# A two-layer hybrid attention and HGRN2 step: one modulation vector moved to VectorE, lower rates of modulation tiles on TensorE, scan and norm steps reordered

## The chip, the core and the metric

The kernel runs on one core of a Trainium2 chip. Its time is the device time of one execution in microseconds (us); for the kernel before, three runs gave 2567.06, 2569.72 and 2571.58, so the median is 2569.72. The profile comes from one further execution.

Five engines have queues of their own: TensorE (PE; its weight loads are listed apart as PEld), VectorE (DVE), ScalarE (ACT), GpSimd (POOL) and SyncE (SP). The last two only issue transfers here.

## What is computed

Two groups of 128 tokens (g = 0, context; g = 1, latent) go through two layers of width 2048. All numbers are float32.

```python
def hybrid_layer(x, mods, ...):
    shift1, scale1, gate1, shift2, scale2, gate2 = mods   # silu(c) @ w_mod[l] + b_mod[l]
    h = modulate(x, shift1, scale1)                       # x * (1 + scale) + shift
    q, k, v, hq, hff, hfb, hi, hgt = split_in(h @ w_in_l)
    att = rms_norm(attend(q, k, v, sink_l), attn_g_l)
    hg, s_f, s_b = hgrn_mixer(hq, hff, hfb, hi, hgt, ...) # two scans over the tokens, in chunks of 32
    mix = jnp.concatenate([att, hg], -1) @ w_o_l
    x = layer_norm(ALPHA * x + gate1 * mix, ln_g_l[0], ln_b_l[0])
    ffn = sq_relu_mlp(modulate(x, shift2, scale2), w_up_l, w_down_l)
    x = layer_norm(ALPHA * x + gate2 * ffn, ln_g_l[1], ln_b_l[1])
```

The six modulation vectors of a layer are numbered v = 0 to 5 in the order shift1, scale1, gate1, shift2, scale2, gate2. Vector (0, 4) is scale2 of the first layer, the scale in front of its MLP. The outputs are x of both groups, the context's k and v, and the final states of both scans.

## The kernel before

**Weight tiles.** Each weight matrix is cut into units of 512 output columns, and a unit into tiles of 512 rows (kg = 0 to 3): 1 MB, loaded as two raw halves of 512 KB by SyncE (L1456) into ten buffers (`RAW_BUFS`). ScalarE rounds each half to float32r (`wh`, L1477), and VectorE subtracts that from the raw half (`wl`, L1490); a product is made of three matmuls, high by high, high by low and low by high. Four buffers each hold `wh` and `wl`, two tiles. Unit kinds are T and N (L462, L477) and W in the MLP (L489, L491); `mm_tile` runs one tile.

**Modulation tiles.** `w_mod` comes in tiles of 1 MB too, 16 for one vector. They are used in two ways. A `Mod` tile goes to TensorE (L204): four float32 matmuls with two stationary columns, which the trace records as eight. `mod_done` then copies the vector from PSUM, transposes it with four matmuls and adds the bias. A `ModH` tile goes to VectorE: four multiply-adds of 128x1024 into two accumulators (L269; the first product of each accumulator, two for a half vector, is ScalarE's, L267). A half vector has eight such tiles. `ModH.done` then sums over the partitions on TensorE with a matmul by ones (L278), copies, and transposes (L305). `POOLED` names the vectors that go the second way. The first layer's vectors 0 and 1 are made in quarters by `ModQ` (L224) ahead of all this.

**The order of the work.** `put_unit` writes a list of work, `seq`: the weight tiles in order, and between them modulation tiles by two credits. After each weight tile `RATE` is added to one credit and `PRATE` to the other, and for each whole credit one tile of `modseq` (TensorE) or of `poolseq` (VectorE) is put into the list:

```python
            pcredit[0] += prate
            while pcredit[0] >= 1.0:
                pcredit[0] -= 1.0
                if poolseq:
                    seq.append(("mod",) + poolseq.popleft())
```

The stages are r1 and r2 (the first and second 512 rows of the first layer's input projection, 13 weight tiles each), in (13 units: 26 tiles in the first layer, 52 in the second), o (two halves of four units with two tiles each: the first over the scan's part of the mix, the second over the attention's) and mlp (four rounds of four up and four down units, 128 tiles). `flush` puts all remaining tiles of the vectors that are needed next into the list at once; vectors 3 and 4 are flushed before the last unit of o. The raw halves are asked for in the order of the list.

**Tasks.** What follows a unit (attention, scans, norms) is written as generators. Each `yield` ends a step; `pump` runs one step of each of the first few admitted tasks, once in the middle of a weight tile and once after it. A task is admitted while at most four PSUM banks are promised. `need` runs steps until a task is done. `scan_task` makes the decayed products of q and k (L793, L794), the matmuls pI (L790), pX in three groups (L813, `across`) and pO. `att_fin` scales the attention output by its RMS (L679), transposes it (L683) and splits it for the output projection.

**The engines' order.** On GpSimd and SyncE the queue has the written order. On the other three a planner orders the instructions ahead of time, by written order among those that its cost model holds ready, so an instruction can stand earlier or later in the queue than where it was written. `ordered` switches to the written order on these three too, in the last tile of a layer half and the first unit after it (the closing). There `hole` puts up to five TensorE modulation tiles into the wait for the norm, and `ln_open` and `ln_mod` normalize and transpose (L973, L993, L1000) four blocks n, one ahead of each weight tile; a modulation tile that stands in the list between these weight tiles comes between these blocks. `ln_out` multiplies the normalized blocks by the norm's gain and adds its bias (L1120, L1121), from rows that GpSimd loads into the two buffers G (L1113, L1114).

## Time and profile before

| | |
|---|---|
| three runs, median (lowest, highest) | 2569.72 us (2567.06, 2571.58) |
| the profiled execution, its own time | 2570.34 us |
| its span, first to last instruction | 2568.6 us |
| mean granted TensorE clock | 0.988 |
| busy: PE, PEld | 2496.6, 2051.5 us |
| busy: DVE, ACT, POOL | 1884.7, 1269.1, 99.3 us |
| moved by DMA | 651.79 MB, mean 254 GB/s |

The span is the time between the first and the last instruction in the trace. Busy is the union of an engine's instructions; a matmul's end is modelled. A wait is idle time of an engine, put down to the instruction that released it. The stages begin, by the first matmul of their first weight tile, at 124.2 us (r2), 219.8 (in), 440.5 (o), 534.9 (second half of o), 596.5 (mlp), 1351.4 (in of the second layer), 1721.7 (o) and 1834.8 (mlp).

### The profile page before, as it was taken

To read this page: it belongs to the slowest core of one execution; us is meant where nothing else is said; L and a number is where in the kernel's file an instruction comes from. 1 tells how busy PE (TensorE), PEld (TensorE's weight loads), DVE (VectorE), ACT (ScalarE), POOL (GpSimd) and SP (SyncE) were. 2 spreads that over 40 slices of the span, in tenths; PEclk is the share of its full clock that TensorE was granted. 3 is DMA by queue.
4 is the path that set the end of the run, shared out by engine and by line. 5 is a ranking of instruction groups with operands and counts; after the bars stand their busy time and mean duration, and the time that the engine had idled before them with its cause. 6 is when DMAs were issued, how large, how long until landed. Compare 5 with 4: busy or idle time off the path is not lost.

```text
span 2568.6 us, 37718 instructions
## 1 busy us (share of the span) xinstructions
PE 2496.6 (97%) x14370; PEld 2051.5 (80%) x14370; DVE 1884.7 (73%) x2496; ACT 1269.1 (49%) x1867; POOL 99.3 (4%) x188
## 2 busy tenths in 40 slices
PE   7999999999999999999999989999999999999998
PEld 4787777668877877878878879797888888888886
DVE  3455787678997977987878788867876565666667
ACT  3434565435545545545535656644554454453552
POOL 2000000100000000000000010001010000000000
PEclk8999999999999999999999999999999999999999
DMA  9888878878887878888877666666666666666663
GB/s 360 283 287 321 293 263 300 288 262 314 312 295 275 309 271 277 293 281 287 278 251 278 205 220 223 209 223 201 207 232 208 225 206 228 209 211 229 205 228 105
DMA packets 192309, 651.79 MB, mean 254 GB/s; under 512 B 22928, under 2 KB 25552, under 8 KB 192128
## 3 DMA queue, kind: packets, MB, share of 16 engines
q1 hardware_dynamic: 177680, 614.56, 68.8%
q0 software_dynamic: 11504, 32.14, 4.2%
q10 hardware_dynamic: 2944, 2.69, 0.3%
q8 instruction: 112, 1.84, 0.3%
q14 instruction: 69, 0.57, 0.1%
HBM read 642.42 MB, written 6.88 MB: 253 GB/s over the span
## 4 chain that ended last, share of the span: by engine, by line
PE 50%; issue 42%; DMA 3%; DVE 3%; POOL 1%; ACT 1%; SPq 0%; DVEq 0%; POOLq 0%; ACTq 0%
PE acc L477 22%; PE acc L462 10%; PE acc L489 8%; PE acc L491 4%; PE psm L204 1%; PE psm L224 1%; DMA G<-in_lng_dram 1%; DMA raw<-in_w_mod_dram 1%; DVE wl L1490 1%; DMA out_nsf_dram<-lf 1%; PE pX L813 1%; POOL G L917 1%; PE pO L851 0%; DVE t L754 0%; PE pI L790 0%
## 5 line engine op out<-in xcount | busy, mean ns | idle before, releaser
L1477 ACT CAST wh<-raw 128x1024 fp32r<-128x1024 f32 x784 | 821.0, 1050 | 992.7 <-PE acc L477 468.7
L1490 DVE TENSOR_TENSOR wl<-raw,wh 128x1024 fp32r<-128x1024 f32 x784 | 951.1, 1220 | 390.1 <-ACT wh L1477 368.3
L269 DVE SCALAR_TENSOR_TENSOR ma<-raw,stat,ma 128x1024 f32<-128x1024 f32 x300 | 378.5, 1278 | 69.3 <-DMA raw<-in_w_mod_dram 68.5
L489 PE MATMUL acc<-ha,wh 128*128 128x512 f32 x960 | 345.5, 399 | 5.6 <-DVE t L1365 5.5
L489 PE MATMUL acc<-hb,wh 128*128 128x512 f32 x960 | 344.2, 398 | 0.0
L477 PE MATMUL acc<-wh,fa 128*128 128x512 f32 x1024 | 342.5, 390 | 0.0
L477 PE MATMUL acc<-wh,fb 128*128 128x512 f32 x1024 | 341.9, 390 | 0.0
L491 PE MATMUL acc<-ha,wl 128*128 128x256 f32 x960 | 269.4, 281 | 0.6 <-DVE wl L1490 0.5
L491 PE MATMUL acc<-hb,wl 128*128 128x256 f32 x960 | 269.4, 281 | 0.2 <-DVE wl L1490 0.2
L477 PEld LDWEIGHTS acc<-wh,fa 128*128 128x128 f32 x1024 | 192.2, 188 | 47.6 <-issue 5.2
L477 PEld LDWEIGHTS acc<-wh,fb 128*128 128x128 f32 x1024 | 192.2, 188 | 43.2 <-issue 3.4
L489 PEld LDWEIGHTS acc<-ha,wh 128*128 128x128 f32 x960 | 180.3, 188 | 56.6 <-DVE t L1365 6.9
L489 PEld LDWEIGHTS acc<-hb,wh 128*128 128x128 f32 x960 | 180.3, 188 | 46.9 <-issue 2.5
L462 PE MATMUL acc<-ha,wh 128*128 128x256 f32 x1152 | 211.7, 288 | 0.4 <-DVE ha L1015 0.4
L462 PE MATMUL acc<-hb,wh 128*128 128x256 f32 x1152 | 211.2, 287 | 0.0
L477 PE MATMUL acc<-wl,fb 128*128 128x512 f32 x512 | 199.5, 390 | 1.5 <-DVE wl L1490 1.5
L477 PE MATMUL acc<-wl,fa 128*128 128x512 f32 x512 | 199.3, 389 | 0.0
L462 PEld LDWEIGHTS acc<-ha,wh 128*128 128x128 f32 x1152 | 177.7, 192 | 25.6 <-issue 15.5
L491 PEld LDWEIGHTS acc<-ha,wl 128*128 128x128 f32 x960 | 181.3, 189 | 1.4 <-DVE wl L1490 1.3
L491 PEld LDWEIGHTS acc<-hb,wl 128*128 128x128 f32 x960 | 181.3, 189 | 0.5 <-DVE wl L1490 0.5
L462 PEld LDWEIGHTS acc<-hb,wh 128*128 128x128 f32 x1152 | 179.4, 195 | 1.3 <-issue 0.8
L462 PE MATMUL acc<-hb,wl 128*128 128x256 f32 x576 | 156.9, 285 | 0.0
(401 smaller groups left out, 3291.2 us busy)
## 6 DMA issues: line engine op xcount, KB each, us to landing
raw<-in_w_mod_dram SPq DMA_DIRECT2D x384, 512.0 KB
raw<-in_w_up_dram SPq DMA_DIRECT2D x256, 512.0 KB
raw<-in_w_down_dram SPq DMA_DIRECT2D x256, 512.0 KB
raw<-in_w_in_dram SPq DMA_DIRECT2D x208, 512.0 KB
raw<-in_w_o_dram SPq DMA_DIRECT2D x64, 512.0 KB
G<-gr POOLq DMA_DIRECT2D x48, 256.0 KB, 4.2
G<-in_lng_dram POOLq DMA_DIRECT2D x12, 256.0 KB, 4.9
G<-in_lnb_dram POOLq DMA_DIRECT2D x12, 256.0 KB, 5.0
```

The source lines that it names most:

```text
L204: pe.matmul(self.ps[32 * j:32 * j + 2, :], lhsT=stat[:, k, :], rhs=raw[j // 2][:, 512 * (j % 2):512 * (j % 2) + 512], start=k == 0, stop=k ...
L224: pe.matmul(self.ps[32 * j:32 * j + 2, :], lhsT=stat[:, 4 * k + j, :], rhs=raw[j // 2][:, 512 * (j % 2):512 * (j % 2) + 512], start=k == 0 ...
L269: dve.scalar_tensor_tensor(self.acc[g], raw[h], c, self.acc[g], ALU.mult, ALU.add)
L462: pe.matmul(ps, lhsT=(wh, wl)[w][k][:, 128 * m:128 * m + 128], rhs=x[:, t], start=f and k == 0 and m % 2 == 0 and (w, t) == (0, 0), stop=e ...
L477: pe.matmul(ps, lhsT=hl[k // 2][:, k % 2, t, gs], rhs=(wh, wl)[w][k], start=f and k == 0 and (t, w) == (0, 0), stop=e and k == ks[-1] == 3 ...
L489: pe.matmul(ps, lhsT=w0, rhs=x.rearrange("p a t -> p (a t)"), start=f and k == 0, stop=False, skip_group_check=True)
L491: pe.matmul(ps[:, 0:256], lhsT=w1, rhs=x[:, 0], start=False, stop=e and k == 3, skip_group_check=True)
L813: pe.matmul(pX[rows(ss), cols(m, ts)], lhsT=kd[:, cols(m, ss)], rhs=qb[:, cols(m, ts)], start=True, stop=True, tile_position=(0, 32 * ss.s ...
L917: side.dma_start(t, gr[g:g + 1, 512 * n:512 * n + 512].partition_broadcast(128))
L1477: act.copy(wh, r)
L1490: dve.tensor_tensor(wl, r, wh.bitcast(F32), ALU.subtract)
```

## The change

Vector (0, 4) joins `POOLED` as its first entry, and `PRATE` of r2, in and o of the first layer rises from 0 to 0.25. `RATE` falls in the first layer (in from 1.2 to 1.0, o from 1.2 to 0.65, mlp from 0.126 to 0.066) and in the second layer's in (0.13 to 0.06). In `scan_task` the two products qb and kd are made a step earlier, ahead of pI, and a step is put between the products at L829 and L830 and the third group of pX. In `att_fin` each block is scaled one block ahead of its transposition. In `ln_out` the rows of a block are loaded ten steps ahead of their use where it was six; the steps before the first block and between the blocks are fewer by as many.

```diff
--- before.py
+++ after.py
@@ -672,11 +672,20 @@
             dve.tensor_tensor(s, ssq[l, g][:, 0:1], ssq[l, g][:, 1:2], ALU.add)
             rs.append(rstd_of(s, 1, 1.0 / 1024, RMS_EPS))
         hls = [new_act("mx"), new_act("mx")]
-        pend = None
+        steps = [(j, g) for j in range(2) for g in range(2)]
+
+        def scaled(i):
+            j, g = steps[i]
+            at = att.pop((l, j, g))
+            dve.tensor_scalar(at, at, rs[g], None, ALU.mult)
+            return at
+
+        ahead = scaled(0)
         for j in range(2):
             for g in range(2):
-                at = att.pop((l, j, g))
-                dve.tensor_scalar(at, at, rs[g], None, ALU.mult)
+                at = ahead
+                if (j, g) != steps[-1]:
+                    ahead = scaled(2 * j + g + 1)
                 yield
                 pt = bank("pt")
                 for h in range(4):
@@ -784,15 +793,15 @@
         dve.tensor_tensor(e2, e2, k, ALU.mult)
         qe, ke = e1, e2
         yield
+        dve.tensor_tensor(eb, eb, q, ALU.mult)
+        dve.tensor_tensor(ed, ed, k, ALU.mult)
+        qb, kd = eb, ed
         yield
         pI = bank("pI")
         for m in range(4):
             pe.matmul(pI[:, 128 * m:128 * m + 128], lhsT=ke[:, 128 * m:128 * m + 128],
                       rhs=qe[:, 128 * m:128 * m + 128], start=True, stop=True)
         yield
-        dve.tensor_tensor(eb, eb, q, ALU.mult)
-        dve.tensor_tensor(ed, ed, k, ALU.mult)
-        qb, kd = eb, ed
         aT = e1
         dve.memset(aT, 0.0)
         mk = "f" if fwd else "b"
@@ -828,6 +837,7 @@
         yield
         dve.tensor_tensor(kdv[:, :, c0], kdv[:, :, c0], dm[:, :, c1:c1 + 1].to_broadcast([128, 4, 32]), ALU.mult)
         dve.tensor_tensor(qbv[:, :, c3], qbv[:, :, c3], dm[:, :, c2:c2 + 1].to_broadcast([128, 4, 32]), ALU.mult)
+        yield
         across(early, late)
         yield
         aTv = v3(aT, 4)
@@ -1106,13 +1116,13 @@
 
     def ln_out(key, li, sink_fn):
 
-        for _ in range(24):
+        for _ in range(20):
             yield
         for n in range(4):
             gt, bt = u("G"), u("G")
             side.dma_start(gt, a["lng"][li:li + 1, 512 * n:512 * n + 512].partition_broadcast(128))
             side.dma_start(bt, a["lnb"][li:li + 1, 512 * n:512 * n + 512].partition_broadcast(128))
-            for _ in range(6):
+            for _ in range(10):
                 yield
             for g in range(2):
                 y = yt.pop((key, n, g))
@@ -1120,16 +1130,16 @@
                     dve.tensor_tensor(y, y, gt, ALU.mult)
                     dve.tensor_tensor(y, y, bt, ALU.add)
                 sink_fn(n, g, y)
-                for _ in range(3):
+                for _ in range(1):
                     yield
 
 
     modseq = deque()
     poolseq = deque()
-    POOLED = ((0, 5), (1, 0), (1, 1), (1, 2), (1, 5))
+    POOLED = ((0, 4), (0, 5), (1, 0), (1, 1), (1, 2), (1, 5))
     ORDER = ['v0 h0 f0 b0 v1 h1 g0 f1 b1 g1 kv q0 q1'] * 2
     PARTS = [((2, 3), (0, 1))] * 2
-    PRATE = {(0, "r1"): 0, (0, "r2"): 0, (0, "in"): 0, (0, "o"): 0, (0, "mlp"): 0.45, (1, "in"): 0.178, (1, "o"): 0.05, (1, "mlp"): 0.135}
+    PRATE = {(0, "r1"): 0, (0, "r2"): 0.25, (0, "in"): 0.25, (0, "o"): 0.25, (0, "mlp"): 0.45, (1, "in"): 0.178, (1, "o"): 0.05, (1, "mlp"): 0.135}
     pcredit = [0.0]
     for l in range(L):
         for v in range(6):
@@ -1428,7 +1438,7 @@
             pump(3)
 
     GAP = 5
-    RATE = {(0, "in"): 1.2, (0, "o"): 1.2, (0, "mlp"): 0.126, (1, "in"): 0.13, (1, "o"): 0.456, (1, "mlp"): 0.066}
+    RATE = {(0, "in"): 1.0, (0, "o"): 0.65, (0, "mlp"): 0.066, (1, "in"): 0.06, (1, "o"): 0.456, (1, "mlp"): 0.066}
     for l in range(L):
         layer(l)
 
```

## Rows read from the trace of the kernel before

**Rows 1.** The page, part 1: busy us (share of the span) xinstructions of each engine.

```profile
PE 2496.6 (97%) x14370; PEld 2051.5 (80%) x14370; DVE 1884.7 (73%) x2496; ACT 1269.1 (49%) x1867; POOL 99.3 (4%) x188
```

**Rows 2.** Windows: stretch, length, PE, PEld, DVE, ACT, POOL busy (x), clock, DMA share, GB/s.

```profile
219.80:440.50 220.70, 214.33 (x1598) 170.45 (x1597) 162.32 (x302) 123.01 (x220) 10.53 (x20) 0.98 0.83 289
...
596.50:1351.40 754.90, 747.83 (x3908) 612.62 (x3908) 638.53 (x684) 373.60 (x476) 15.60 (x30) 1.00 0.83 287
1351.40:1721.70 370.30, 355.60 (x2560) 318.23 (x2560) 301.29 (x482) 226.23 (x392) 16.21 (x30) 0.98 0.66 228
```

**Rows 3.** Waits of PE: who <- for whom: us in total, times, longest us.

```profile
PE pX L813 <- DVE ed L830: 10.3, 2, 7.3
...
PE acc L489 <- DVE t L1365: 5.5, 3, 3.4
...
PE pt L683 <- DVE q L679: 4.1, 2, 2.2
...
PE pX L813 <- DVE s L824: 2.9, 2, 1.9
...
PE pt L993 <- DVE Z L973: 2.7, 1, 2.7
```

**Rows 4.** Timeline of PE: start, us, instruction, count [idle before <- releaser].

```profile
332.46 0.56 PE L813 MATMUL pX<-ed,t 128*32 128x32 f32 x16 [1.86 <-DVE s L824]
```

**Rows 5.** Windows after two holes.

```profile
333.00:336.40 3.40, 3.40 (x17) 3.40 (x17) 3.40 (x9) 0.63 (x1) 0.00 (x0) 0.50 0.51 188
...
1503.80:1514.00 10.20, 5.37 (x28) 5.25 (x29) 10.04 (x19) 3.18 (x8) 0.00 (x0) 0.50 0.43 153
```

**Rows 6.** Timeline of PE in the first layer's input projection.

```profile
245.71 0.28 PE L462 MATMUL acc<-hb,wl 128*128 128x256 f32 x1
245.92 1.04 PE L204 MATMUL psm<-raw,stat 128*2 128x512 f32 x8
246.89 0.50 PE L462 MATMUL acc<-ha,wh 128*128 128x256 f32 x2
247.23 0.28 PE L462 MATMUL acc<-ha,wl 128*128 128x256 f32 x1
247.35 0.40 PE L462 MATMUL acc<-ha,wh 128*128 128x256 f32 x2
...
252.62 0.28 PE L462 MATMUL acc<-hb,wl 128*128 128x256 f32 x1
252.83 1.90 PE L204 MATMUL psm<-raw,stat 128*2 128x512 f32 x16
254.65 0.50 PE L462 MATMUL acc<-ha,wh 128*128 128x256 f32 x2
```

**Rows 7.** Instructions by line and shape: xcount | busy us, mean ns | idle before.

```profile
L269 DVE SCALAR_TENSOR_TENSOR ma<-raw,stat,ma 128x1024 f32<-128x1024 f32 x300 | 378.5, 1278 | 69.3 <-DMA raw<-in_w_mod_dram 68.5 <-ACT ma L267 0.7
...
L278 PE MATMUL ph<-ma,ones 128*32 128x512 f32 x80 | 10.7, 605 | 0.0
...
L305 PE MATMUL pt<-ident,w 128*128 128x128 f32 x16 | 2.4, 272 | 0.0
```

**Rows 8.** Window of L204 alone: PE, PEld busy (x), clock, DMA share, GB/s.

```profile
514.60:534.30 19.70, 8.39 (x48) 1.06 (x48) 1.00 0.92 341
```

**Rows 9.** Windows of all instructions, columns as in rows 2.

```profile
369.00:392.50 23.50, 23.48 (x144) 16.07 (x140) 23.06 (x46) 15.16 (x29) 0.00 (x0) 1.00 0.81 282
...
534.90:579.60 44.70, 44.70 (x211) 34.54 (x210) 33.15 (x53) 16.41 (x20) 3.23 (x6) 0.97 0.71 228
...
650.00:700.00 50.00, 50.00 (x276) 42.10 (x275) 48.76 (x54) 27.11 (x38) 3.04 (x6) 1.00 0.87 310
```

**Rows 10.** Timeline of DVE in the second layer's first unit.

```profile
1358.95 4.86 DVE L269 SCALAR_TENSOR_TENSOR ma<-raw,stat,ma 128x1024 f32<-128x1024 f32 x4
```

**Rows 11.** Waits of DVE.

```profile
DVE Z L1120 <- DMA G<-in_lng_dram: 6.7, 2, 3.4
```

**Rows 12.** DMA issues: engine op xcount, KB each, median us to landing.

```profile
G<-in_lng_dram POOLq DMA_DIRECT2D x12, 256.0 KB, 4.9
```

## The prediction

> **What bounds the kernel now.** The busy line comes first: TensorE works for 2496.6 of 2568.6 us and VectorE for 1884.7 [rows 1]. The reader is to see that the time is TensorE's work plus some 70 us of holes. The windows by stage come next [rows 2]. Window length minus PE busy gives the idle time: 6.4 us in the first layer's input projection (219.8 to 440.5), 7.1 us in its MLP, 14.7 us in the second layer's input projection. VectorE is 74%, 85% and 81% busy there: no bound on average, but little is left. The list of TensorE's waits names the holes [rows 3]: nearly all wait for VectorE, and two of them (pX at L813) are what the scan edits touch. The last view is the clock. A hole of 1.86 us before 332.46 [rows 4] is followed by 3.4 us at a granted clock of 0.50 [rows 5], the lower level, 1.2 GHz. TensorE is busy for all of that stretch and does half the work, so such a hole costs 1.7 us more than its length. After the longest wait on L830, 7.3 us, the low clock lasts from 1503.8 to 1514.0 with 5.37 us busy in it [rows 5], which is 2.7 us lost.
>
> **The change, part by part.** The sum is made against the profiled execution: 2570.34 us, its span of 2568.6 and 1.74 around it. It lies 0.6 us above the median of the three runs, 2569.72.
>
> *Tiles that leave TensorE.* A modulation tile is eight matmul records. Between two weight tiles, the next weight matmul starts 1.18 us after the last one (245.71 to 246.89), and 0.12 us is its step without a tile (247.23 to 247.35): 1.06 us for one tile. Two together take 254.65 - 252.62 - 0.12 = 1.91 us, so the second costs 0.85 and each separate run of tiles 0.21 more [rows 6]. Vector (0,4) has 16 tiles. Following the rates through the list of work, 80 tiles in 64 runs become 64 in 55: 16 x 0.85 + 9 x 0.21 = 15.5 us. Back come two sums over partitions, each eight records of 80, 10.7 / 10 = 1.07 us, and four more transposes, 0.6 us (16 took 2.4): +2.7 [rows 7]. Not all of it was on the path. From 514.6 to 534.3 TensorE waits for a chain of attention steps, and 48 records, six tiles, lie in the gaps [rows 8]. By the order of the list some four can still be pulled in there: two tiles of saving are lost, +2. Together -10.8 (ends: -12.8, all on the path, and -7.7, all six worth nothing).
>
> *What VectorE gets.* (0,4) adds 64 multiply-adds, of which four run on ScalarE: 60 x 1.278 = 76.7 us [rows 7]. At 0.25 for a weight tile, 13 + 26 + 12 weight tiles give 12.75, so twelve tiles come before the last unit of the output projection; the flush puts the other four in one lump before it: 16 x 1.278 = 20.4 us of VectorE. Raw tiles are consumed in that order, so the low part of the last unit's first weight tile (L1490, on VectorE) stands behind the lump, TensorE's last unit behind that, and only the unit before gives TensorE work meanwhile. From 534.9 to 579.6 VectorE now works for 33.2 of 44.7 us [rows 9]. With three modulation tiles gone TensorE needs about 42, so VectorE has 9 us to spare and 11.4 are late; some of the lump may run earlier, in the holes of the attention chain (ends: 0, and 20.4 with the low part's two instructions, 22.8). I take 9 us of stall and 1.7 for the clock, nearest to the 11.4: +11 (0 to 26). Of the twelve tiles before, six fall into the input projection and three into the output projection, where VectorE is full in places: 23.06 of 23.5 us from 369.0 [rows 9]. The nearest row for so full a VectorE is the MLP from 650 to 700, 48.76 of 50 us busy and TensorE without a hole [rows 9]. So I take only +4 (0 to 15).
>
> *The scan.* The products qb and kd are made one step earlier, and the third group of pX matmuls is issued one step later. A step is half a weight tile, 2.7 us or more (eight weight tiles and their modulation tiles fill the 50 us from 650). The waits on L824 (2.9 us) go with one clock loss of 1.7; of the two waits on L830 (10.3 us [rows 3]) the shorter, 3.0, falls to about nothing with its 1.7, the longer loses 2.9: 4.6 + 4.7 + 2.9, -12 (0 to -21, all these holes and their clock losses). What is late next is the scan itself: each of 16 tasks takes a step more, four pairs in a row in each layer, and the task that sums (0,4) takes a bank from them for some steps. That lies beside weight tiles, except before the first layer's output projection, where the chain is already waited for: +5 (0 to 10).
>
> *Attention scale one tile ahead.* The waits at L683 (4.1 us [rows 3]) end when L679 does, and L679 needs the row statistics of the last head group, which are no earlier now. I cost the edit at 0 (1 to -4). In the second layer, though, eight modulation tiles now lie in the output projection where none were, and one or two fill a wait: -2.
>
> *The closings.* The first unit after each norm is in a fixed order. A multiply-add tile after its first weight tile (4.86 us at 1358.95 [rows 10]) stands before VectorE's norm work, and TensorE waits 2.7 us at L993 [rows 3] plus 1.7 of clock. The credit carried over moves such a tile from the second layer's input projection to the first layer's MLP, there with half the VectorE work (its first products are ScalarE's): -2 (-4.4 to +3).
>
> *Norm rows.* VectorE waits 6.7 us at L1120 for rows [rows 11], with all that is queued behind; the 3.4 us TensorE hole at L489 [rows 3] is in such a stretch. Four steps more of lead lower the priority of these products, but the two buffers of G still let the next rows start only after the last products: -3 (-6 to +3). A row lands 4.9 us after its issue [rows 12]. The Trainium skill ("DMA: Bandwidth & Descriptors", Anatomy of one DMA) gives 2.0 us and the bytes by 436 GB/s for this queue, 2.6 us for 256 KB as an estimate; by that no row would be late after six steps, this part would be 0 and the sum 3 us higher. The trace differs from it, and decides.
>
> Sum: -10.8 + 11 + 4 - 12 + 5 + 0 - 2 - 2 - 3 = -9.8, so 2570.34 - 9.8 = 2560.5; I say 2560.
>
> **The rivals.**
> *VectorE's lump decides (slower).* The multiply-adds stand ahead of the weight splits in VectorE's order and nothing covers them: the four tiles of the flush cost 22.8, three more in full stretches of the input projection 3 x 5.1 = 15.3, four clock losses 7: +45 where I have +15, thus 2590. It makes the kernel slower once stalls and clock losses of this kind pass 25 us, which is what the other parts give. For it: 33.2 of 44.7 us before the lump is added. Against it: the window from 650, where 98% leaves no hole.
> *Fillers and holes come back (no change).* The tiles only filled waits (-7.7 for -10.8) and the longer scan chain eats its gain (-2 net for -7): 2560.5 + 3 + 5 = 2568.5. For it: six tiles in the gaps of 19.7 us [rows 8]. Against it: the tiles at 245.92 and 252.83 stand between weight tiles with no hole beside them [rows 6].
> *The lump is covered (faster).* Flush 0 for 11, scan -17 for -12, rows -6 for -3: 2541.5.
> *The rows are not asked earlier at all*, since the G buffers set it: 3 us, inside the others' ranges.
>
> **How the numbers follow.** My forecast has 0.45 (2548 to 2573), the covered lump 0.15, no change 0.22, slower 0.18. About 0.2%, 5 us, is what a measurement of this kernel can tell from no change: 2564.6 and 2574.9. Of the forecast's 0.45, 0.31 is faster, 0.11 within, 0.03 slower; of no change's 0.22, 0.11, 0.08 and 0.03: faster 0.57, same 0.19, slower 0.24. The range runs from 2535, where more of the scan's end is added to the covered lump, to 2584, most of the way to the slower case.
>
> **What would show it.** L204 has 512 records and L269 360. A hole before the last unit of the first output projection with L1490 as what ended it, about 9 us: far over 15 and the first rival holds, none and the third does. No wait on L824 at L813, and less than 5 us on L830. L993 without 2.7 us in the second layer's input projection. TensorE's busy time falls by 12 to 15; if idle time rises by as much, it was filler. The forecast is wrong if the idle time from 219.8 to 534.9 doubles, or if the span falls by over 30.

## The result and the profile after

The changed kernel takes 2586.23 us (median of five runs, 2581.18 to 2588.74) where the kernel before takes 2569.72 (2567.06 to 2572.41). The ratio is 1.0058, 95% interval 1.0041 to 1.0074: slower by 0.6%, some 15 us. The forecast was 2560, its range ended at 2584. Where us stand beside a ratio below, they are its distance from 1, times 2570.

The page's first part of the changed kernel answers to [rows 1]. TensorE is busy 6.5 us less, VectorE 65.8 us more, and the span is 18.4 us longer: TensorE's idle time rose.

```profile
PE 2490.1 (96%) x14262; PEld 2048.3 (79%) x14262; DVE 1950.5 (75%) x2555; ACT 1272.2 (49%) x1872; POOL 99.3 (4%) x188
```

The windows of the changed kernel, columns as in [rows 2], are cut at the first weight matmul of each stage: input projection, first and second half of the output projection (the second also in two parts), MLP, the second layer's input and output projections.

```profile
218.40:447.10 228.70, 213.16 (x1538) 166.55 (x1537) 183.79 (x303) 124.85 (x216) 10.54 (x20) 0.98 0.82 285
447.10:564.70 117.60, 95.58 (x499) 65.22 (x495) 82.09 (x165) 44.26 (x115) 7.48 (x14) 0.91 0.68 234
564.70:633.30 68.60, 58.24 (x276) 41.30 (x273) 59.33 (x88) 20.98 (x30) 4.30 (x8) 0.93 0.74 232
...
564.70:599.00 34.30, 34.30 (x159) 28.13 (x157) 33.40 (x45) 13.74 (x17) 2.15 (x4) 1.00 0.72 222
599.00:633.30 34.30, 23.94 (x118) 13.17 (x116) 25.93 (x44) 7.25 (x13) 2.15 (x4) 0.85 0.76 242
...
633.30:1378.70 745.40, 739.86 (x3853) 612.85 (x3853) 643.62 (x688) 374.41 (x476) 15.65 (x30) 1.00 0.81 281
1378.70:1736.40 357.70, 347.55 (x2525) 315.27 (x2525) 294.06 (x470) 223.53 (x391) 16.16 (x30) 1.00 0.66 223
1736.40:1856.30 119.90, 114.65 (x567) 87.17 (x563) 85.53 (x150) 48.40 (x89) 11.75 (x22) 0.99 0.76 255
```

The output projection of the kernel before, which stands in no row so far:

```profile
440.50:534.90 94.40, 90.44 (x507) 59.94 (x503) 63.73 (x128) 41.01 (x106) 7.49 (x14) 1.00 0.86 299
534.90:596.50 61.60, 58.36 (x291) 41.86 (x289) 42.33 (x75) 21.02 (x30) 4.30 (x8) 0.95 0.76 251
```

Length against [rows 2] and these: +8.0 in the first input projection, +23.2 and +7.0 in the two halves of its output projection, -9.5 in the MLP, -12.6 in the second input projection, +6.8 in the second output projection (1721.7 to 1834.8 before), where 68 matmul records more run, modulation tiles that the lower rates leave for this stage. Of the 45.0 us by which stages grow, 38.2 lie in the first layer ahead of its MLP. In the first half of the output projection the granted clock falls from 1.00 to 0.91 as well: PE is busy 5.1 us longer there with eight records fewer.

The waits of TensorE in the changed kernel answer to [rows 3] (L822, L839 and L1003 are L813, L830 and L993 of before):

```profile
PE pX L822 <- DVE ed L839: 9.5, 4, 5.9
PE ph L278 <- DVE ma L269: 8.4, 1, 8.4
...
PE pt L1003 <- DVE Y L983: 4.7, 1, 4.7
```

Two of these are the largest holes. The first is at 458.0, behind two modulation tiles (four records are one raw half of a tile):

```profile
456.95 1.03 PE L204 MATMUL psm<-raw,stat 128*2 128x512 f32 x4 [0.25 <-DMA raw<-in_w_mod_dram]
463.84 1.12 PE L822 MATMUL pX<-ed,t 128*64 128x64 f32 x8 [5.86 <-DVE ed L839]
...
608.00 1.89 PE L278 MATMUL ph<-ma,ones 128*32 128x512 f32 x2 [8.36 <-DVE ma L269]
```

The second is the lump, and VectorE shows what it waits for: the last multiply-adds, at the end of a stretch without a gap.

```profile
593.42 3.68 DVE L269 SCALAR_TENSOR_TENSOR ma<-raw,stat,ma 128x1024 f32<-128x1024 f32 x3
...
601.20 1.28 DVE L269 SCALAR_TENSOR_TENSOR ma<-raw,stat,ma 128x1024 f32<-128x1024 f32 x1
602.39 0.69 DVE L933 BATCH_NORM_STATS2 bs<-Y 128x6 f32<-128x512 f32 x1
602.99 6.06 DVE L269 SCALAR_TENSOR_TENSOR ma<-raw,stat,ma 128x1024 f32<-128x1024 f32 x5
608.96 3.50 DVE L1500 TENSOR_TENSOR wl<-raw,wh 128x1024 fp32r<-128x1024 f32 x3
```

The scan chain falls behind as it goes. Below, the pI matmuls of the first layer's eight scan tasks, of the kernel before and of the changed one (min/median/max ns, first to last start): they begin 1.2 us later and end 26.7 us later. TensorE's own work is later too: its output projection begins at 447.1 for 440.5, 6.6 us later.

```profile
L790 PE MATMUL pI<-e,lf x64: 275/275/348, 274.3 to 445.7; 128*128 128x128 f32 x64
```

```profile
L802 PE MATMUL pI<-e,lf x64: 270/275/378, 275.5 to 472.4; 128*128 128x128 f32 x64
```

### The profile page after: what moved, and what is told of

The parts are those of the page before. It is cut to its first block, busy times and chain, and to the rows that moved or that the text cites. A ratio compares the mean times of both kernels' runs of the same rounds, so it can differ in the third digit from the quotient of the medians.

```text
span 2587.0 us, 37567 instructions
## 1 busy us (share of the span) xinstructions
PE 2490.1 (96%) x14262; PEld 2048.3 (79%) x14262; DVE 1950.5 (75%) x2555; ACT 1272.2 (49%) x1872; POOL 99.3 (4%) x188
## 4 chain that ended last, share of the span: by engine, by line
PE 76%; DVE 10%; issue 7%; DMA 6%; ACT 1%; SPq 0%; POOL 0%; DVEq 0%; ACTq 0%; POOLq 0%
PE acc L477 31%; PE acc L489 17%; PE acc L462 13%; PE acc L491 8%; DMA raw<-in_w_mod_dram 3%; DVE wl L1500 3%; DVE ma L269 2%; PE psm L204 2%; PE psm L224 1%; DMA out_nsf_dram<-lf 1%; PE pO L861 1%; PE pX L822 1%; DMA raw<-in_w_in_dram 0%; DMA G<-in_lng_dram 0%; ACT wh L1487 0%
## 5 line engine op out<-in xcount | busy, mean ns | idle before, releaser
L1500 DVE TENSOR_TENSOR wl<-raw,wh 128x1024 fp32r<-128x1024 f32 x784 | 952.7, 1222 | 346.9 <-ACT wh L1487 322.9
L269 DVE SCALAR_TENSOR_TENSOR ma<-raw,stat,ma 128x1024 f32<-128x1024 f32 x360 | 454.6, 1282 | 59.7 <-DMA raw<-in_w_mod_dram 58.3
L491 PE MATMUL acc<-hb,wl 128*128 128x256 f32 x960 | 269.3, 281 | 0.0
L491 PE MATMUL acc<-ha,wl 128*128 128x256 f32 x960 | 268.8, 281 | 0.0
L462 PEld LDWEIGHTS acc<-ha,wh 128*128 128x128 f32 x1152 | 176.7, 192 | 28.2 <-issue 16.9
L462 PE MATMUL acc<-ha,wl 128*128 128x256 f32 x576 | 155.6, 284 | 1.5 <-DVE wl L1500 1.5
```

Source lines behind the costliest of these rows:

```text
L269: dve.scalar_tensor_tensor(self.acc[g], raw[h], c, self.acc[g], ALU.mult, ALU.add)
L462: pe.matmul(ps, lhsT=(wh, wl)[w][k][:, 128 * m:128 * m + 128], rhs=x[:, t], start=f and k == 0 and m % 2 == 0 and (w, t) == (0, 0), stop=e ...
L491: pe.matmul(ps[:, 0:256], lhsT=w1, rhs=x[:, 0], start=False, stop=e and k == 3, skip_group_check=True)
L1500: dve.tensor_tensor(wl, r, wh.bitcast(F32), ALU.subtract)
```

## The experiments

Theory 1: the extra step of the scan tasks delays the first layer's chain. Theory 2: VectorE's time for (0,4), between 132 and 609 us, delays it. The end of the chain is told by the start of the last pF, a late matmul of a scan task: 455.7 us in the kernel before, 481.4 in the changed one. The first four runs take the parts of the change apart; lines of code that don't matter here are left out of the cuts, with dots.

**The changed kernel with the old scan task.**

```
-        dve.tensor_tensor(eb, eb, q, ALU.mult)
-        dve.tensor_tensor(ed, ed, k, ALU.mult)
-        qb, kd = eb, ed
         yield
         pI = bank("pI")
...
+        dve.tensor_tensor(eb, eb, q, ALU.mult)
+        dve.tensor_tensor(ed, ed, k, ALU.mult)
+        qb, kd = eb, ed
         aT = e1
...
-        yield
         across(early, late)
```

> The changed kernel with the scan task as it was before (qb and kd made after the pI matmuls, no extra step ahead of the third pX group); constants, attention scale and norm rows stay changed. Theory 1 (the extra step of the eight scan tasks delays the first layer's scan chain, and the output projection waits for it): the last pF of the first layer goes back from 481 to about 455-460 us, idle time in the first output projection from 22 to under 8 us, the time to 2560-2572 us although the pX waits of the second layer come back (+5 to +10). Theory 2 (VectorE's multiply-adds of (0,4) between 95 and 560 us delay the chain; the scan edit by itself gains): the last pF stays near 481 us and the time goes to 2588-2600 us.

Measured: 2580.85 us, ratio 1.0039 (1.0023 to 1.0055). Last pF at 471.8. Neither answer came: without the scan edit the time falls by 0.0019, 4.9 us, where theory 1 wanted 14 or more and theory 2 a rise. From the start of the input projection to the MLP it is 11 us shorter than the changed kernel, in the second layer's input projection 4.5 longer.

**The kernel before with the new scan task alone** (the diff above the other way round).

> The kernel before with the scan edit alone (products one step earlier, third pX group one step later). Theory 1: the first layer's last pF moves from 455 to about 475-481 us and the first output projection gains 15-20 us of length; with 8-12 us gained in the second layer the time is 2574-2584 us. Theory 2: the last pF moves by under 6 us, the pX waits go, 2556-2564 us.

Measured: 2560.49, ratio 0.9959 (0.9945 to 0.9973): -10.5 us. Last pF 459.6. Theory 2 is right here in the time and in the chain's end, but not in that the pX waits go. The extra step has its price all the same. The windows below are the input projection from the unit v1 on, 11.5 us shorter than before (the last line, of the kernel before), the first half of the output projection, 10.7 longer, and the second input projection, 10.3 shorter.

```profile
277.00:428.40 151.40, 150.10 (x1144) 118.33 (x1140) 114.23 (x221) 86.00 (x159) 10.55 (x20) 1.00 0.85 296
428.40:533.50 105.10, 92.00 (x537) 62.45 (x534) 73.53 (x158) 45.08 (x116) 7.48 (x14) 0.97 0.79 278
1349.10:1709.10 360.00, 353.09 (x2560) 316.19 (x2561) 300.06 (x482) 225.72 (x392) 16.18 (x30) 1.00 0.71 236
...
277.60:440.50 162.90, 156.67 (x1176) 123.79 (x1172) 124.16 (x251) 90.23 (x170) 10.53 (x20) 0.98 0.82 281
```

The wait on L830 is about as large as before (10.3 us in [rows 3]), and 7.9 us of it now lies in the output projection:

```profile
PE pX L813 <- DVE ed L830: 9.8, 3, 7.9
```

**The kernel before with the constants alone**: the lines `POOLED`, `PRATE` and `RATE` of the change, nothing else.

> The kernel before with the three lines of constants alone (POOLED with (0,4), PRATE, RATE). Theory 1: the first layer's last pF stays within 6 us of 455, the cost is the lump before the last unit only, 2557-2570 us. Theory 2: the last pF moves to 470-481 us, the idle time from 219.8 us to the end of the first output projection rises from 13.6 to over 35 us, 2580-2595 us.

Measured: 2590.45, ratio 1.0078 (1.0065 to 1.0092): +20.0 us, last pF 473.8. The constants make the loss, more than all of it. TensorE's idle time from 218.4 to 552.8 is 28.2 us (13.6 + 14.6), and with the stage of the lump 39. Its windows (input projection, the two halves of the output projection):

```profile
218.40:446.10 227.70, 214.15 (x1562) 167.16 (x1561) 186.75 (x305) 123.24 (x213) 10.55 (x20) 0.99 0.82 285
446.10:552.80 106.70, 92.10 (x474) 61.79 (x471) 80.92 (x163) 45.74 (x118) 7.48 (x14) 0.95 0.76 260
552.80:621.20 68.40, 57.38 (x276) 40.68 (x273) 59.33 (x88) 20.96 (x30) 6.26 (x12) 0.95 0.75 237
```

**The kernel before with attention scale and norm rows alone**: the edits of `att_fin` and `ln_out` in the change, nothing else.

> The kernel before with the attention scale one tile ahead and the norm rows asked for ten steps ahead, without the scan edit and the constants. Theories 1 and 2 both: 2564-2571 us (0 from the first, -3 from the second), no stage of the first input or output projection longer by over 3 us. Theory 3 (these edits, moving VectorE work of the norm and the attention against the rest, hold a good part of the loss): 2576-2586 us.

Measured: 2568.68, ratio 0.9985 (0.9971 to 0.9999), -3.9 us. These edits are not the loss. On top of the constants they are worth more: the constants alone have 1.0078, the constants with these edits (the run with the old scan task) 1.0039, 10.0 us less, of which 6.3 show in the second layer's input projection (368.5 and 362.2 us long).

**The constants with thin multiply-adds of (0,4).** This kernel leaves out most of the sum.

```
+n = 8 if (self.l, self.v) == (0, 4) else 1024
-dve.scalar_tensor_tensor(self.acc[g], raw[h], c, self.acc[g], ...)
+dve.scalar_tensor_tensor(self.acc[g][:, 0:n], raw[h][:, 0:n], c, self.acc[g][:, 0:n], ...)
```

> The three constant lines alone, and the multiply-adds of (0,4) on VectorE cut to 8 of their 1024 columns (the rest of that sum is left out); order of the list, tasks, banks and transfers are those of the constants alone (2590 us, ratio 1.0078). Theory 2 (VectorE's time for (0,4) delays the scan chain and makes the hole before the last unit): 2554-2564 us, last pF of the first layer back from 474 to 455-460 us, no hole of over 2 us before the last unit. Theory 4 (not the time but the list: fewer TensorE tiles to cover waits, the closing task in front of the scan tasks, its bank): 2582-2592 us, last pF stays at 470 us or later.

Measured: 2560.53, ratio 0.9957 (0.9943 to 0.9971). With the same list, tasks and transfers, VectorE's time for (0,4) alone is worth 0.0121, 31 us. Its windows beside those of the constants are 9.6, 3.7 and 9.4 us shorter.

```profile
218.90:437.00 218.10, 210.44 (x1562) 169.34 (x1562) 161.18 (x312) 122.20 (x212) 10.58 (x20) 0.98 0.87 299
437.00:540.00 103.00, 88.90 (x468) 61.33 (x467) 71.46 (x155) 45.72 (x118) 7.50 (x14) 0.96 0.76 263
540.00:599.00 59.00, 56.72 (x279) 41.08 (x277) 43.89 (x88) 21.02 (x30) 6.28 (x12) 0.98 0.82 282
```

One part missed: the last pF is at 462, not 455 to 460, and the first half of the output projection stays 8.6 us longer than before.

**The old RATE with the sums on VectorE** (POOLED and PRATE as changed).

> POOLED and PRATE as changed, RATE as before: (0,4) on VectorE, and as many TensorE tiles (48) ahead of the last unit of the first output projection as before, so the filler there is that of before. Theory 2: the loss stays, 2583-2597 us, last pF at 470 us or later. Theory 4, by its part on fillers (35 tiles instead of 48 leave waits uncovered): idle time in the first output projection back under 6 us, 2562-2574 us.

Measured: 2602.36, ratio 1.0117 (1.0099 to 1.0135), last pF 482.4, idle time in the first half of the output projection 14.8. With more TensorE tiles the idle time there is what it was with fewer (14.6 in the constants alone). That answer of theory 4 falls.

**No lump** (0.315 for 0.25 in PRATE).

> The three constant lines with 0.315 for 0.25 in the first layer's PRATE: all 16 tiles of (0,4) are summed before the last units, none is left in one lump. Beside 2590 us for the constants alone: if the lump costs what its hole shows (8 us and a clock loss), 2578-2584 us, the hole of 8 us at L278 gone; by theory 2 the four tiles cost in the projections instead what they cost at the end, the chain is 3-6 us later still and the time is 2583-2592 us. A cover of the load without loss would give 2565 us.

Measured: 2601.51, ratio 1.0113 (1.0094 to 1.0131), outside all three answers. Against the constants alone the last unit of the output projection shrinks by 16.0 us (34.1 to 18.1, second line below), but the input projection grows by 22.3 (227.7 to 250.0, first line): the four tiles are dearer in that stage than in the lump.

```profile
219.70:469.70 250.00, 225.16 (x1595) 174.34 (x1594) 200.03 (x334) 132.23 (x229) 10.57 (x20) 0.94 0.79 273
...
611.00:629.10 18.10, 17.52 (x108) 11.58 (x104) 13.03 (x27) 5.42 (x11) 1.62 (x3) 1.00 0.87 286
```

**The two halves of the scan edit**, each on the kernel before: products early; extra step alone.

> The kernel before with half of the scan edit: the products qb and kd one step earlier, without the extra step ahead of the third pX group. Both halves together measured 2560.5 us, ratio 0.9959. If the earlier products make the gain and the extra step only delays the chain: the first input projection 8-12 us shorter as with both, the first output projection under 100 us long instead of 105, 2552-2559 us. If the extra step makes the gain (L830's waits): 2565-2572 us.

> The kernel before with the other half of the scan edit: the third pX group a step later, the products qb and kd where they were. The early products alone measured 0.9999. If the extra step makes the gain by itself: 2557-2563 us, waits on L830 under 4 us, those on L824 as before. If the two halves only gain together: 2565-2572 us. If the extra step costs by itself (a longer chain): 2573-2580 us.

Measured: 2570.97, ratio 0.9999 (0.9985 to 1.0012), and 2564.45, ratio 0.9988 (0.9979 to 0.9997). Early products alone give nothing; the step alone gives 3 us, less than it was to give if it made the gain by itself; only both give 10.5.

**All edits to the code, no constants.**

> The kernel before with all the edits to the code (scan, attention scale, norm rows) and none of the constants. If the parts add: -10.4 (scan, measured) and -3.9 to 0 (attention and norm rows, measured ratio 0.9985), 2553-2562 us, ratio 0.993 to 0.997. If the scan edit's gain and that of the norm rows are the same waits: as the scan edit alone, ratio 0.996 or above.

Measured: 2555.86, ratio 0.9953 (0.9941 to 0.9965). Within the intervals the parts add (-10.5 and -3.9 for -12.1), and this is faster than both kernels.

**The sums ahead of the scan chain**, on the constants, and on the changed kernel.

```
-PRATE (0,"r1"): 0,   (0,"r2"): 0.25, (0,"in"): 0.25, (0,"o"): 0.25
+PRATE (0,"r1"): 0.6, (0,"r2"): 0.65, (0,"in"): 0,    (0,"o"): 0
```

> The three constant lines with the sums of (0,4) moved ahead of the scan chain: 0.6 a weight tile in the first pass over the first quarter of rows, 0.65 in the second pass (VectorE there 54% busy), none in the input and output projections. Theory 2 (it is the place beside the scan chain that costs, not the sum itself): the last pF of the first layer at 455-462 us, no hole before the last unit, 2556-2568 us. Rival (transfers: 16 MB more in 187 us in which the 16 DMA engines are already 80 to 90% busy): the two passes grow by 15-30 us, 2570-2590 us. If VectorE's sum costs its 23-30 us wherever it lies: 2585-2595 us.

> The run with the sums ahead of the scan chain, and the edits of scan, attention scale and norm rows as well, thus the changed kernel with another place for the sums. Theory 2: 2543-2558 us, faster than both kernels. By the transfers rival 2558-2580 us.

Measured: 2603.41, ratio 1.0135 (1.0122 to 1.0148), and 2591.2, ratio 1.0090 (1.0075 to 1.0105). Both times lie above every answer that was given. The two passes grow by what the rival, transfers, gave them; that transfers are the cause is not shown, since the multiply-adds themselves stand in these passes too. The two passes of the first run:

```profile
32.90:133.60 100.70, 91.95 (x584) 76.13 (x584) 77.77 (x93) 41.99 (x60) 11.40 (x19) 0.93 0.97 352
133.60:246.80 113.20, 104.17 (x689) 79.73 (x689) 90.62 (x107) 33.82 (x43) 0.00 (x0) 0.96 0.92 334
```

and the same two of the kernel before:

```profile
33.10:124.20 91.10, 88.66 (x592) 72.93 (x592) 49.45 (x69) 42.87 (x58) 11.39 (x19) 0.97 0.89 312
124.20:219.80 95.60, 94.87 (x660) 75.57 (x657) 52.06 (x69) 33.30 (x42) 0.00 (x0) 0.98 0.86 304
```

They grow by 27.2 us; the DMA share of the first goes from 0.89 to 0.97, and TensorE loses clock. Of TensorE's 17.8 us of idle time in them, 6.7 end with ScalarE's rounding of a weight half and 6.5 with VectorE's low part. Behind them the chain is near the old one: last pF 490.6, 243.8 us after the input projection's start (235.9 before, 255.4 with the constants). The second run is 0.0045 below the first: with the sums out of the chain's way, and `RATE` as changed, the edits to the code gain 11.6 us, about what they gain on the kernel before.

**The changed kernel with thin multiply-adds; the lump alone whole** (the first twelve tiles thin: `(self.l, self.v) == (0, 4) and (self.h, k) < (1, 4)`, on the constants).

> The changed kernel whole, with the multiply-adds of (0,4) on VectorE cut to 8 of 1024 columns (the rest of that sum is left out). If the other terms of the forecast hold, without the +11 and +4 for VectorE's time, it says 2545; by the runs so far 0.9957 x 0.9953 = 0.991, 2545-2550 us. If the scan edit's gain is lost to the fewer TensorE tiles and not to VectorE's load: 2556-2566 us.

> The three constant lines with the first twelve tiles of (0,4) cut to 8 columns and the last four, the lump, whole. Between 2560.5 us (all sixteen cut) and 2590.4 us (none cut). As the forecast had it (lump 11, elsewhere 4 of 15, scaled to the 30 measured: 22 and 8): 2578-2585 us. If the twelve beside the scan chain decide: 2562-2570 us.

Measured: 2562.08, ratio 0.9982 (0.9968 to 0.9995), and 2571.93, ratio 1.0009 (0.9997 to 1.0020). The second splits VectorE's price: the lump 0.0052, 13.4 us; the twelve tiles 0.0069, 17.7 us. That is neither of the two answers, but between. The first says that the rest of the sum does not hold either: even without VectorE's load the edits to the code, which gain 12 us on the kernel before, cost 0.0025, 6 us, on the new constants (the intervals of 0.9957 and 0.9982 touch). With the load they gain 0.0020, 5 us (1.0078 to 1.0058). No run takes them apart on thin multiply-adds.

**Without the extra step in the second head group of the first layer**, on all edits to the code, and on the changed kernel.

```
-        yield
+        if (l, G) != (0, 1):
+            yield
         across(early, late)
```

> The kernel before with all edits to the code and no constants (2555.9 us, ratio 0.9953), without the extra step in the four scan tasks of the first layer's second head group (l, G) = (0, 1). If those four steps are what the output projection waits for, and the input projection's gain comes from the first head group: the first output projection 95-98 us long instead of 105, ratio 0.990 to 0.993. If the gain and the wait hang on the same four tasks: the input projection is 8-11 us longer again, ratio 0.994 to 0.997.

> The changed kernel without the extra step in the four scan tasks of the first layer's second head group. If their steps cost what the run without the scan edit gained in the first output projection (10 us): 2576-2581 us, last pF from 481 to 472 us. If the steps of the first head group, or the earlier products, are what delays the chain under load: 2583-2589 us.

Measured: 2557.78, ratio 0.9942 (0.9924 to 0.9960), no profile of it is read; and 2583.49, ratio 1.0055 (1.0041 to 1.0069), last pF 475.4. The first can't be told from 0.9953, the second not from 1.0058: in the time these four steps show no price, though in the profile of the second the MLP begins 3.9 us earlier.

**The scan edit in the second layer only; old RATE with thin multiply-adds**, both on the changed kernel.

> The changed kernel with the scan edit in the second layer only. If its price lies in the first layer (11 us from the start of the input projection to the MLP, by the run without it) and its gain in the second (4 to 12 us): 2572-2579 us, the first layer as in the run without the edit (MLP from 622 us), the second layer's input projection at 358 us. If the second layer's gain is only the later start of the first: 2579-2584 us.

> The changed kernel with the multiply-adds of (0,4) cut to 8 columns (the rest of that sum is left out) and RATE as before, so 48 TensorE tiles lie ahead of the last unit of the first output projection instead of 35. With the new RATE it measured 0.9982. If the fewer tiles turn the scan edit's sign: ratio 0.990 to 0.994, 2544-2554 us, idle time in the first output projection under 13 us. If the tiles are only work that comes back elsewhere: 0.996 to 1.000.

Measured: 2577.1, ratio 1.0020 (1.0007 to 1.0034), MLP from 622.6 us; and 2561.37, ratio 0.9962 (0.9949 to 0.9976), idle time in the first half of the output projection 15.4. The first is as expected. Against the run with the old scan task the second layer gains 0.0019, 5 us; against the changed kernel the first layer's edit costs 0.0038, 10 us. The second misses the answer by which the tiles decide and lies at the edge of the other: that it is the number of TensorE tiles that turns the scan edit's sign is not borne out.

## Why the prediction was wrong

**The step that failed first: "So I take only +4 (0 to 15)" for VectorE's fullness outside the lump.** The twelve tiles measure 17.7 us. The constants as a whole were forecast at about 0 (-10.8 + 11 + 4 - 2 - 2) and measure +20.0. The row that I leaned on was the MLP's window of 50 us with 98% VectorE and no hole [rows 9]; the constants alone and the run with thin multiply-adds show that it is the wrong neighbour. In the input projection 25.6 us more of VectorE (161.18 to 186.75) make the stage 9.6 us longer at a mean load of 82%. Of these, 3.7 us are busy time of TensorE and 5.9 idle time. The largest part of the idle time is a wait that the sum had no term for, that of a modulation tile of TensorE for its raw half. The lines below are of this stage, of the constants alone and of thin multiply-adds:

```profile
PE psm L204 <- DMA raw<-in_w_mod_dram: 6.7, 3, 2.8
...
PE psm L204 <- DMA raw<-in_w_mod_dram: 0.8, 1, 0.8
```

Waits for a weight half's two parts (L1477, L1490) are 2.7 us for 0.3; those of the scan tasks and their ends (L790, L813, L900) are 4.1 for 6.7, so they are no larger. The three waits for a tile lie between 369 and 381 us, where VectorE is busy for nearly all of the time and the DMA engines are full:

```profile
355.00:381.00 26.00, 19.32 (x135) 11.64 (x134) 24.77 (x33) 15.55 (x34) 0.48 (x1) 0.93 0.98 360
```

SyncE waits 21.0 us in this stage for multiply-adds at L269 before it issues a raw half (14.8 with thin ones): a multiply-add that stands late in VectorE's order holds its raw buffer, and the transfers behind it begin late. That this is the way from VectorE's time to the tile's wait is read from these waits; no run with more buffers tests it. The kernel before has such waits too, elsewhere:

```profile
PE psm L224 <- DMA raw<-in_w_mod_dram: 9.7, 8, 5.2
```

The prediction's reading that nearly all holes wait for VectorE passed over it.

The same work also stands inside the chain of dependent steps. The changed kernel's VectorE between the scan instruction and the product for pI of the fifth task:

```profile
376.59 1.22 DVE L761 TENSOR_TENSOR_SCAN t<-rmask,lf 128x512 f32<-128x512 f32 x1
377.72 1.26 DVE L269 SCALAR_TENSOR_TENSOR ma<-raw,stat,ma 128x1024 f32<-128x1024 f32 x1
378.90 0.69 DVE L772 TENSOR_TENSOR e<-t 128x512 f32<-128x512 f32 x1
379.50 0.69 DVE L773 TENSOR_TENSOR ed<-t 128x512 f32<-128x512 f32 x1
380.10 1.28 DVE L269 SCALAR_TENSOR_TENSOR ma<-raw,stat,ma 128x1024 f32<-128x1024 f32 x1
381.30 0.69 DVE L793 TENSOR_TENSOR lf<-lf,pa 128x512 f32<-128x512 f32 x1
381.90 0.69 DVE L792 TENSOR_TENSOR e<-e,pa 128x512 f32<-128x512 f32 x1
```

Two multiply-adds, 2.4 us, lie inside one step of the chain. But against TensorE's own work the chain is not later for it in the constants alone: the last pI of the first layer starts at 462.8 with whole multiply-adds and at 453.7 with thin ones, in both 16.7 us after the output projection begins (446.1 and 437.0), and at the same place in TensorE's order. What ends TensorE's waits in this stage differs between runs with the load: without the lump, a tile's raw half ends 10.1 us of them and steps of the scan tasks 8.3; with the old `RATE`, 6.7 us lie before one transposition of the scan's output (L900), and none before a raw half. What these runs show in common is that VectorE's time costs, not by which wait.

```profile
L790 PE MATMUL pI<-e,lf x64: 271/275/348, 275.5 to 462.8; 128*128 128x128 f32 x64
```

```profile
L791 PE MATMUL pI<-e,lf x64: 270/275/585, 269.3 to 453.7; 128*128 128x128 f32 x64
```

**The second: the scan, "-12" and "+5 (0 to 10)".** On the kernel before the edit measures -10.5, near the -7 of the sum, but not by the waits I named. The wait on L830 did not shrink; it moved into the output projection (7.9 of 9.8). "No wait on L824" was right, "less than 5 us on L830" wrong (9.5). In the changed kernel the edit measures +4.9 (1.0039 to 1.0058): +9.8 in the first layer, -4.9 in the second. The late chain costs what the end of my range said, 10.7 us in the output projection of the kernel before and 9.8 net in the changed one; what is missing there is the first layer's gain, and half of the second's; the rest of the second's is already there in the run with the old scan task (362.2 us for 368.5). (The intervals of 1.0039 and 1.0020 overlap, and those of 1.0039 and 1.0058; the MLP's start, 622.4 and 622.6 against 633.3 us, says the same for the first layer.) The order of TensorE's work shows a part of how. Counted from the traces, the weight tile behind which the pI matmuls of the last four scan tasks stand (the units in order: g1, kv, q0, q1 with tiles 2 and 3, then o), and their start:

```
kernel                  5th            6th            7th            8th
before                  g1.3 380.0     kv.3 397.0     q1.2 422.1     o.2 445.0
before, new scan        kv.2 381.7     kv.3 389.6     o.2  431.3     o.2 450.6
constants alone         g1.3 397.8     q0.2 415.6     q1.3 440.9     o.2 462.1
constants, thin sums    g1.3 386.5     q0.2 406.5     q1.3 431.7     o.2 452.9
changed kernel          kv.2 403.9     q0.2 417.4     o.2  450.0     o.2 471.5
sums ahead of the chain g1.3 413.0     kv.3 429.2     q1.2 457.3     o.2 476.0
```

The scan edit moves the fifth and the seventh task back; the constants move the sixth and the seventh, in each of the ten runs in which the closing of (0,4)'s first half (ph, at 396.4 us in the changed kernel, at 382 with thin sums) stands behind g1.3. Where it stands at 144.7 us, the places are the old ones. In the changed kernel the last two tasks stand inside and behind o.2, the last weight tile that doesn't wait for them. From there only modulation tiles lie between the steps, and the holes are the chain's own: 5.86 us before the third pX group, four more of 1 to 1.6. Of the thin run's 14.1 us of idle time in this stage, 5.0 are of this kind and 3.7 a wait for a modulation tile.

The places do not explain the sign of the scan edit by themselves. By the table the scan edit alone puts the last two tasks behind q1.3 as well, with a hole of 7.9 us there, and still gains, since its input projection is 11.5 us shorter; with the constants only the sixth task, at q0.2 for kv.3, stands later than with the scan edit alone. And in the run without the lump, where that closing stands behind f1.3, no place is later than in the kernel before, but the last pF starts at 483.1. The number of tiles on TensorE does not explain the sign either: the last run did not bring the gain back with more of them, and with the sums ahead of the chain, where they are as few, the edits to the code cost the first layer nothing (377.4 us from the input projection to the MLP with them, 377.9 without; 414.8 and 404.0 in the changed kernel and the run with the old scan task). On the constants with thin sums they do cost it (387.8 and 380.1). Between these two pairs it is (0,4)'s tiles, their transfers and their closing inside the stage that differ; which of them takes the first layer's gain stays open.

**Right or nearly.** The lump: forecast +11, measured 13.4 (the lump alone whole, less all thin), its hole 8.36 us for 9. What ended it was not L1490, though, but the last multiply-adds, through the sum over partitions, L278, which stands in TensorE's order ahead of the last unit's low part (that part, L1500 at 608.96 above, comes right behind the lump). The tiles that leave TensorE, with the fillers and closings: -14.8 forecast, -11.1 measured (the constants, all thin), in which the late places are contained. TensorE's busy time falls by 12.1 us with the load away (2484.5 in that run), 6.5 in the changed kernel, at a lower mean clock (0.989 and 0.986). L204 has 512 records and L269 has 360. The 2.7 us at L993 in the second layer are gone; the 4.7 us in the list belong to another tile. Attention and rows together: -3 forecast, -3.9 measured on the kernel before, but not by the rows' waits. In that run VectorE waits 18.2 us for rows where the kernel before has 17.3, so the reason given for -3 is not borne out:

```profile
DVE Z L1129 <- DMA G<-in_lng_dram: 7.7, 2, 4.7
DVE Y L1130 <- DMA G<-in_lnb_dram: 6.4, 3, 2.8
DVE Y L1129 <- DMA G<-in_lng_dram: 4.1, 2, 3.5
```

The wait of 3.5 us shows why: the row is issued at 700.5, 0.2 us after the last product of the block before begins, and lands at 705.6, when its own product starts. There the buffers of G set the issue, as the prediction's last rival has it, and not the number of steps. With the constants the waits do fall, to 12.3 us, and with both to 12.6 in the changed kernel.

The Trainium skill's figure for such a row ("DMA: Bandwidth & Descriptors", Anatomy of one DMA) has it land 2.6 us after its issue, as the prediction's estimate. The trace does not agree: the median of that run is 5.0 us (12 rows).

**The sum of it.** Taken in the order constants, attention and rows, scan, the steps measure +20.0, -10.0 and +4.9, which is +14.9. The forecast had +0.2, -3 and -7, which is -9.8.

**The rivals.** The slower one, VectorE's lump at 2590, came nearest, with 45 us for VectorE where 31 were measured. It had lump and full stretches as one mechanism; its chance of 0.18 was too small because I took one full but quiet stretch of VectorE for evidence on stages with other waits. My own sign of failure (TensorE's idle time from 219.8 to 534.9 doubling) came true: 10.3 us before, 37.6 from 218.4 to 564.7.

Not everything adds. In the changed kernel VectorE's time costs 19.5 us (1.0058 less 0.9982), not 31; that the chain is late there anyway may be why, which no run tests.

## What to carry to other kernels

Work that is moved to an engine with room on average is priced by what waits for that engine in the same stage, not by the busy share, and not by another stage that happens to be full and quiet. Ask two things of the stage itself: how many of the moved instructions fall between two steps of a chain, and which buffers they hold, since the transfers behind them begin only when these come free. A step added to a chain of tasks costs where the list of covering work ends; find, in the bound engine's order, the last piece of work that doesn't wait for the chain, and see which steps fall behind it. When a change has a part in the code and a part in constants, the two can differ in sign: here the code alone is 0.5% faster (0.9953) and the constants alone 0.8% slower. And an edit's worth on the kernel before need not be its worth beside the others: the scan edit gives -10.5 us alone and +4.9 as the last of the parts.

## What the runs showed beside this

Moving the sums to the start, where VectorE is 54% busy, was the dearest version of all (1.0135): with about seven of the sixteen tiles in it the first pass has the DMA engines at a share of 0.97 for 0.89, at 352 GB/s, and TensorE idle for 8.8 us at a granted clock of 0.93, for 2.4 us at 0.97. A multiply-add over 8 columns took 0.15 to 0.22 us in most records, against 1.28 us over 1024 (in this line of the thin run from 120 to 640 us, 60 of 71 records are of 8 columns, and the longest is one of 1024):

```profile
L270 DVE SCALAR_TENSOR_TENSOR ma<-raw,stat,ma x71: 154/222/1280, 133.4 to 639.3; 128x8 f32<-128x8 f32 x60, 128x1024 f32<-128x1024 f32 x11
```
